# A batched matmul with hardware loops on ScalarE and VectorE, and transfer completions passed on by GpSimd

## The chip, the cores and the metric

One core of one Trainium2 chip. The metric is the device time of the whole kernel in microseconds (us), lower is better.

## The reference

```python
batch, m, k, n = 16, 512, 512, 512          # a: (16,512,512) f32, b: (16,512,512) f32
def reference(a, b):
    return np.matmul(a, b.transpose(0, 2, 1)).astype(np.float32)
```

Inputs are 33.55 MB, the output 16.78 MB, all f32 in HBM.

## The kernel before

The sixteen products are worked in eight pairs. SP loads `a` and `b` of a pair (2 MiB each) into seven slots; VectorE casts each load to bf16 in two halves (`h` and `w`), TensorE transposes both through PSUM, ScalarE copies the transposed `a` out (`ta`), VectorE the transposed `b` (`tb`), TensorE multiplies, ScalarE copies the result to one of seven output slots (`ob`), and SP stores it (1 MiB). TensorE already runs a hardware loop. ScalarE and VectorE are unrolled; each wait names an absolute count. Store 0 alone goes out from ScalarE's own transfer queue (q10 in the page: 1.05 MB).

```python
ORDER = "LLLLLLLSLLLLSLSSLSLSLLSSSSSSSSS"    # SP: L = a load, S = a store (from store 1 on)
# ... SP
if n_ld >= NL:
    nc.sync.wait_ge(s_cd, n_ld - NL + 1)     # the slot's last cast is done
# ... the first two loads come in two halves; VectorE casts half by half
# VectorE, unrolled over pairs u
nc.vector.wait_ge(s_ld[n % NL], 16 * (n // NL + 1))
nc.vector.wait_ge(s_t, KO * u)
nc.vector.tensor_copy(out=h[:], in_=src[:, :, :HK]).then_inc(s_c, 1)
nc.vector.tensor_copy(out=w[:], in_=src[:, :, HK:]).then_inc(s_cd, 1)
# ... then ha<-wa, tb, hb<-wb, tb, tb, tb
# ScalarE, unrolled over pairs
nc.scalar.wait_ge(s_mm, J * i + j + 1)
c = nc.scalar.copy(out=ob[i % NO][:, j, :]..., in_=ps[:, j, :]...)
if i == 1 and j == 0:
    nc.scalar.wait_ge(s_out, 1)
    nc.scalar.dma_start(out[0]..., ob[0][:]).then_inc(s_st[0], 16)
```

Of the kernel before, what the change touches and what calls it, by code (L numbers as in the profile page):

```python
# [10 lines left out]
def kernel(  # L11
# [6 lines left out]
    nc = tc.nc  # L18
    P = 128
    batch, M, K = a.shape  # L20
    _, N, _ = b.shape
    J = M // P
    KO = K // P
    HP = P // 2
    HK = K // 2
    pairs = batch // 2
    f32 = mybir.dt.float32
    bf16 = mybir.dt.bfloat16
    NL = 7
    NO = 7  # L30


    ORDER = "LLLLLLLSLLLLSLSSLSLSLLSSSSSSSSS"

    def sbuf(name, shape, dtype):
        return ctx.enter_context(nc.sbuf_tensor(name, shape, dtype))

    def sem(name):
        return tc.alloc_semaphore(name)

    with tc.tile_critical(no_gpsimd_drain=True):  # L41
        ident = sbuf("ident", [P, P], bf16)
        ld = [sbuf(f"ld{i}", [P, 2 * J, K], f32) for i in range(NL)]
        ha, wa, hb, wb = (
            sbuf(name, [P, 2 * J, HK], bf16) for name in ("ha", "wa", "hb", "wb")
        )
        ta = sbuf("ta", [P, KO, 2 * J * P], bf16)
        tb = sbuf("tb", [P, KO, 2 * J * P], bf16)
        ob = [sbuf(f"ob{i}", [P, J, N], f32) for i in range(NO)]
        tp = ctx.enter_context(nc.psum_tensor("tp", [P, 4, 2 * J, P], bf16))  # L50
        ps = ctx.enter_context(nc.psum_tensor("ps", [P, 4, N], f32))

# [1 line left out]
        s_ld = [sem(f"s_ld{i}") for i in range(NL)]  # L54
        s_second = [sem(f"s_second{i}") for i in range(2)]
        s_st = [sem(f"s_st{i}") for i in range(NO)]
        s_cd = sem("s_cd")
        s_ca = sem("s_ca")
        s_cb = sem("s_cb")
        s_ta = sem("s_ta")  # L60
        s_tb = sem("s_tb")
        s_ea = sem("s_ea")
        s_eb = sem("s_eb")
        s_mm = sem("s_mm")
        s_pv = sem("s_pv")
        s_out = sem("s_out")
# [5 lines left out]
            out=ident[:], in_=ident[:], compare_op=mybir.AluOpType.not_equal, fill=1.0,  # L72
# [4 lines left out]



        n_ld, n_st = 0, 1  # L80
        for what in ORDER:
            if what == "L":
                u, slot = n_ld // 2, n_ld % NL
                src = (a if n_ld % 2 == 0 else b)[2 * u:2 * u + 2].rearrange(
                    "e (p j) k -> (e p) j k", j=2 * J
                )
                if n_ld >= NL:

                    nc.sync.wait_ge(s_cd, n_ld - NL + 1)
                if n_ld < 2:  # L90
                    nc.sync.dma_start(
                        ld[slot][:, :J, :], src[:, :J, :]
                    ).then_inc(s_ld[slot], 16)
                    nc.sync.dma_start(
                        ld[slot][:, J:, :], src[:, J:, :]
                    ).then_inc(s_second[slot], 16)
                else:
                    nc.sync.dma_start(ld[slot][:], src).then_inc(s_ld[slot], 16)
                n_ld += 1
            else:  # L100
                slot = n_st % NO
                nc.sync.wait_ge(s_out, n_st + 1)
                nc.sync.dma_start(
                    out[n_st].rearrange("(p j) n -> p j n", j=J), ob[slot][:]
                ).then_inc(s_st[slot], 16)
                n_st += 1
        for n in range(batch - NO, batch - 1):
            nc.sync.wait_ge(s_st[n % NO], 16 * (n // NO + 1))




        nc.vector.nop().then_inc(s_eb, 2)
        nc.vector.wait_ge(s_set, 2)
        both = ((ha, wa, s_ca, s_ta), (hb, wb, s_cb, s_tb))
        for u in range(pairs):
            for x, (h, w, s_c, s_t) in enumerate(both):
                n = 2 * u + x
                src = ld[n % NL]
                nc.vector.wait_ge(s_ld[n % NL], 16 * (n // NL + 1))  # L120
                nc.vector.wait_ge(s_t, KO * u)
                if n >= 2:
                    nc.vector.tensor_copy(out=h[:], in_=src[:, :, :HK]).then_inc(s_c, 1)  # L123
                    nc.vector.tensor_copy(out=w[:], in_=src[:, :, HK:]).then_inc(s_cd, 1)  # L124
                else:
                    nc.vector.tensor_copy(out=h[:, :J, :], in_=src[:, :J, :HK])  # L126
                    nc.vector.tensor_copy(out=w[:, :J, :], in_=src[:, :J, HK:])  # L127
                    nc.vector.wait_ge(s_second[n], 16)
                    nc.vector.tensor_copy(  # L129
                        out=h[:, J:, :], in_=src[:, J:, :HK]  # L130
                    ).then_inc(s_c, 1)
                    nc.vector.tensor_copy(  # L132
                        out=w[:, J:, :], in_=src[:, J:, HK:]
                    ).then_inc(s_cd, 1)
            for ko in range(KO):
                if ko < 2:
                    h, w, s_c, s_t = both[ko]
                    nc.vector.wait_ge(s_cd, 2 * u + ko + 1)
                    nc.vector.wait_ge(s_t, KO * u + 2)
                    nc.vector.tensor_copy(out=h[:], in_=w[:]).then_inc(s_c, 1)  # L140
                nc.vector.wait_ge(s_tb, KO * u + ko + 1)
                nc.vector.tensor_copy(  # L142
                    out=tb[:, ko, :],
                    in_=tp[:, 2 + ko % 2].rearrange("k j p -> k (j p)"),
                ).then_inc(s_eb, 1)


        nc.scalar.nop().then_inc(s_ea, 2)
        for u in range(pairs):
            for ko in range(KO):  # L150

                nc.scalar.wait_ge(s_ta, KO * u + ko + 1)
                for e in range(2):
                    c = nc.scalar.copy(  # L154
                        out=ta[:, ko, e * J * P:(e + 1) * J * P].rearrange(
                            "k (j p h) -> k j p h", j=J, h=2
                        ),
                        in_=tp[:, ko % 2, :, e * HP:(e + 1) * HP].rearrange(
                            "k (h j) p -> k j p h", h=2
                        ),  # L160
                    )
                c.then_inc(s_ea, 1)
            for e in range(2):
                i = 2 * u + e
                if i >= NO:
                    nc.scalar.wait_ge(s_st[i % NO], 16 * (i // NO))
                for j in range(J):
                    nc.scalar.wait_ge(s_mm, J * i + j + 1)

                    c = nc.scalar.copy(  # L170
                        out=ob[i % NO][:, j, :].rearrange("m (p j) -> m p j", j=2 * J),
                        in_=ps[:, j, :].rearrange("m (j p) -> m p j", j=2 * J),
                    )
                    if j == J - 1:
                        c.then_inc(s_out, 1)
                    elif e == 0 or j == 0:
                        c.then_inc(s_pv, 1)
                    if i == 1 and j == 0:
                        nc.scalar.wait_ge(s_out, 1)
                        nc.scalar.dma_start(  # L180
                            out[0].rearrange("(p j) n -> p j n", j=J), ob[0][:]
                        ).then_inc(s_st[0], 16)


        def take(s, n):
            nc.tensor.wait_ge(s, n).then_inc(s, -n)  # L186

        pe = nc.tensor.engine
        with nc.Fori(0, pairs, engines=[pe]):
            with nc.Fori(0, 2, engines=[pe]):  # L190

                for x, (h, s_c, s_t, s_e) in enumerate(
                    ((ha, s_ca, s_ta, s_ea), (hb, s_cb, s_tb, s_eb))
                ):
                    take(s_c, 1)
                    for g in range(2):
                        take(s_e, 1)
                        for j in range(2 * J):
                            t = nc.tensor.transpose(  # L199
                                tp[:, 2 * x + g, j, :], h[:, j, g * P:(g + 1) * P], ident[:]  # L200
                            )
                        t.then_inc(s_t, 1)
            nc.tensor.wait_ge(s_ea, 2)
            nc.tensor.wait_ge(s_eb, 2)


            for e in range(2):
                for j in range(J):
                    if e == 1 and j % 2 == 0:
                        take(s_pv, 2)  # L210
                    for ko in range(KO):
                        t = nc.tensor.matmul(  # L212
                            ps[:, j, :],
                            ta[:, ko, (e * J + j) * P:(e * J + j + 1) * P],
                            tb[:, ko, :].rearrange("k (j p) -> k j p", j=2 * J)[
                                :, :, e * HP:(e + 1) * HP
                            ],
                            start=(ko == 0),
                            stop=(ko == KO - 1),
                        )  # L220
                    t.then_inc(s_mm, 1)
# [34 lines left out]
```

## Time and profile before

| | before |
|---|---|
| time, median of the first 3 runs | 126.25 us |
| span of the profiled run | 124.3 us |
| busy: TensorE, VectorE, ScalarE | 74%, 55%, 57% |
| transfer engines | 9 tenths in all slices but the first and the last two |
| last output copy ends | 115.43 us |
| last store: issued, landed on the slowest engine | 115.46, 123.02 us |

In the profile's rows PE is TensorE (PEld its weight loads), DVE VectorE, ACT ScalarE, POOL GpSimd and SP SyncE; a q behind the name (SPq, DVEq) is the engine's sequencer or queue, L129 a line of the kernel. Each transfer runs in sixteen parts on sixteen transfer engines (each of the 34 issues in this trace has sixteen landing records). "Landing" is the record that a part has arrived, and "rings" are the queues in which issued transfers wait for the engines: the median store of this trace lands 24.7 us after its issue.

The rows that carry this are shown in the prediction. The two columns to hold side by side are the last two lines of the table: compute ends 7.6 us before the transfers do.

Two rows of the timeline show how the first pair starts (columns: start us, length us, engine, line, operation, output from input, count, idle time before it and what ended it):

```profile
8.52 0.69 DVE L129 CAST ha<-ld 128x1024 bf16<-128x1024 f32 x1 [1.11 <-DMA ld<-in_a_dram]
14.70 0.69 DVE L140 COPY ha<-wa 128x2048 bf16<-128x2048 bf16 x1
```

The second half of the first `a` landed at 8.49 us, so its cast begins 0.03 us later.

### The profile page before, as it was taken

Reading aid. Unit: us, or ns where it says so; the run is one execution under the profiler, and the core shown is the slowest. Engines: PE = TensorE matmul, PEld = TensorE weight load, DVE = VectorE, ACT = ScalarE, POOL = GpSimd, SP = SyncE. Lnnn points to the kernel's source line nnn. Section 1 sums busy time; section 2 is a strip of 40 time slices with the busy share of each in tenths; the row PEclk is TensorE's granted clock in tenths of the full one; section 3 lists DMA queues with packets and bytes.
Section 4 is the critical chain, followed back from the end, with each engine's and each line's share of the span. In section 5 each row is a group of like instructions: output and inputs, shape, how many; then the busy total and the mean of one; then the engine's idle time right before and its main releaser. Section 6 shows DMA issues by size and latency. Waiting matters only on the chain. (4 is left out here: it accounts for less than half of the span.)

```text
span 124.3 us, 2076 instructions
## 1 busy us (share of the span) xinstructions
PE 91.8 (74%) x768; PEld 56.5 (45%) x768; DVE 67.9 (55%) x84; ACT 71.0 (57%) x129; POOL 0.7 (1%) x6
## 2 busy tenths in 40 slices
PE   0005397998699869986998699869986998699000
PEld 0005394447444744574447444744474447443000
DVE  0065668827891788278907890782686568400000
ACT  4006042769476946694669476947694769476100
POOL 2000000000000000000000000000000000000000
PEclk9999999999999999999999999999999999999955
DMA  3999999999999999999999999999999999999980
GB/s 79 403 427 451 443 427 427 427 427 374 411 427 424 445 432 443 424 422 430 414 430 406 416 451 387 403 451 416 448 427 422 419 422 427 427 427 427 424 377 34
DMA packets 4898, 50.35 MB, mean 405 GB/s; under 512 B 544, under 2 KB 544, under 8 KB 544
## 3 DMA queue, kind: packets, MB, share of 16 engines
q1 hardware_dynamic: 4752, 49.29, 94.5%
q10 hardware_dynamic: 144, 1.05, 2.0%
q14 instruction: 2, 0.02, 0.0%
HBM read 33.55 MB, written 16.78 MB: 405 GB/s over the span
## 5 line engine op out<-in xcount | busy, mean ns | idle before, releaser
L212 PE MATMUL ps<-tb,ta 128*128 128x512 bf16 x256 | 57.3, 379 | 8.0 <-DVE tb L142 8.0
L170 ACT COPY ob<-ps 128x512 f32<-128x512 f32 x64 | 37.6, 587 | 30.1 <-PE ps L212 30.1
L212 PEld LDWEIGHTS ps<-tb,ta 128*128 128x128 bf16 x256 | 23.9, 97 | 39.0 <-ACT ta L154 8.2
L154 ACT COPY ta<-tp 128x512 bf16<-128x512 bf16 x64 | 32.9, 604 | 13.3 <-PE tp L199 12.9
L199 PE MATMUL tp<-ident,ha 128*128 128x128 bf16 x256 | 19.7, 230 | 11.8 <-PEq L186 10.9
L199 PEld LDWEIGHTS tp<-ident,ha 128*128 128x128 bf16 x256 | 16.7, 104 | 15.5 <-issue 13.8
L142 DVE COPY tb<-tp 128x1024 bf16<-128x1024 bf16 x32 | 21.3, 685 | 3.9 <-PE tp L199 3.6
L199 PE MATMUL tp<-ident,hb 128*128 128x128 bf16 x256 | 18.5, 230 | 3.1 <-PEq L186 3.1
L199 PEld LDWEIGHTS tp<-ident,hb 128*128 128x128 bf16 x256 | 16.3, 104 | 3.4 <-issue 3.3
L140 DVE COPY ha<-wa 128x2048 bf16<-128x2048 bf16 x8 | 5.5, 693 | 18.1 <-PE tp L199 18.1
L123 DVE CAST hb<-ld 128x2048 bf16<-128x2048 f32 x7 | 8.6, 1226 | 7.2 <-DMA ld<-in_b_dram 7.2
L123 DVE CAST ha<-ld 128x2048 bf16<-128x2048 f32 x7 | 8.5, 1219 | 0.6 <-DMA ld<-in_a_dram 0.6
L124 DVE CAST wb<-ld 128x2048 bf16<-128x2048 f32 x7 | 8.5, 1221 | 0.0
L124 DVE CAST wa<-ld 128x2048 bf16<-128x2048 f32 x7 | 8.5, 1220 | 0.0
L140 DVE COPY hb<-wb 128x2048 bf16<-128x2048 bf16 x8 | 5.5, 685 | 0.2 <-PE tp L199 0.2
L126 DVE CAST ha<-ld 128x1024 bf16<-128x1024 f32 x1 | 0.7, 694 | 6.1 <-DMA ld<-in_a_dram 6.1
L154 ACT ACT_TABLE_LOAD x1 | 1.3, 1283 | 1.0 <-SPq L41 1.0
L129 DVE CAST hb<-ld 128x1024 bf16<-128x1024 f32 x1 | 0.7, 694 | 1.2 <-DMA ld<-in_b_dram 1.2
L126 DVE CAST hb<-ld 128x1024 bf16<-128x1024 f32 x1 | 0.7, 695 | 1.2 <-DMA ld<-in_b_dram 1.2
L129 DVE CAST ha<-ld 128x1024 bf16<-128x1024 f32 x1 | 0.7, 694 | 1.1 <-DMA ld<-in_a_dram 1.1
L132 DVE CAST wa<-ld 128x1024 bf16<-128x1024 f32 x1 | 0.7, 689 | 0.0
L127 DVE CAST wa<-ld 128x1024 bf16<-128x1024 f32 x1 | 0.7, 687 | 0.0
(8 smaller groups left out, 2.3 us busy)
## 6 DMA issues: line engine op xcount, KB each, us to landing
out_dram<-ob SPq DMA_DIRECT2D x15, 1024.0 KB, 25.8
ld<-in_a_dram SPq DMA_DIRECT2D x7, 2048.0 KB, 30.8
ld<-in_b_dram SPq DMA_DIRECT2D x7, 2048.0 KB, 30.5
ld<-in_a_dram SPq DMA_DIRECT2D x2, 1024.0 KB, 6.1
ld<-in_b_dram SPq DMA_DIRECT2D x2, 1024.0 KB, 10.1
out_dram<-ob ACTq DMA_DIRECT2D x1, 1024.0 KB, 12.2
```

The lines of the kernel that those rows point to most:

```text
L123: nc.vector.tensor_copy(out=h[:], in_=src[:, :, :HK]).then_inc(s_c, 1)
L124: nc.vector.tensor_copy(out=w[:], in_=src[:, :, HK:]).then_inc(s_cd, 1)
L126: nc.vector.tensor_copy(out=h[:, :J, :], in_=src[:, :J, :HK])
L127: nc.vector.tensor_copy(out=w[:, :J, :], in_=src[:, :J, HK:])
L129: nc.vector.tensor_copy(out=h[:, J:, :], in_=src[:, J:, :HK]).then_inc(s_c, 1)
L132: nc.vector.tensor_copy(out=w[:, J:, :], in_=src[:, J:, HK:]).then_inc(s_cd, 1)
L140: nc.vector.tensor_copy(out=h[:], in_=w[:]).then_inc(s_c, 1)
L142: nc.vector.tensor_copy(out=tb[:, ko, :], in_=tp[:, 2 + ko % 2].rearrange("k j p -> k (j p)"),).then_inc(s_eb, 1)
L154: c = nc.scalar.copy(out=ta[:, ko, e * J * P:(e + 1) * J * P].rearrange("k (j p h) -> k j p h", j=J, h=2), in_=tp[:, ko % 2, :, e * HP:(e ...
L170: c = nc.scalar.copy(out=ob[i % NO][:, j, :].rearrange("m (p j) -> m p j", j=2 * J), in_=ps[:, j, :].rearrange("m (j p) -> m p j", j=2 * J),)
L199: t = nc.tensor.transpose(tp[:, 2 * x + g, j, :], h[:, j, g * P:(g + 1) * P], ident[:])
L212: t = nc.tensor.matmul(ps[:, j, :], ta[:, ko, (e * J + j) * P:(e * J + j + 1) * P], tb[:, ko, :].rearrange("k (j p) -> k j p", j=2 * J)[:, ...
```

## The change

The intent is a much smaller program for ScalarE and VectorE: one loop body each instead of eight copies. This loop body is the same code for every pair and names neither the semaphore of a slot nor a growing count, so GpSimd waits for the real completions in issue order and passes them on as plain counts (`s_go` for loads, `s_of` for free output slots), and each consumer takes its count back off the semaphore. Slots are addressed from a register. A tiny copy ahead of ScalarE's loop is to make the activation table load there and not in the loop. Store 0 is issued once, ScalarE's loop body runs for every pair, so it moves to SP's queue, ahead of store 1.

```diff
-    ORDER = "LLLLLLLSLLLLSLSSLSLSLLSSSSSSSSS"
+    ORDER = "LLLLLLLSSLLLLSLSSLSLSLLSSSSSSSSS"
-        n_ld, n_st = 0, 1
+        n_ld = n_st = 0
-                    nc.sync.wait_ge(s_cd, n_ld - NL + 1)
+                    nc.sync.wait_ge(s_cd, n_ld - NL + 2)
 # GpSimd, new
+        for what in ORDER:
+            if what == "L":
+                if n_ld < 2:
+                    nc.gpsimd.wait_ge(s_second[n_ld], 16)
+                nc.gpsimd.wait_ge(s_ld[n_ld % NL], 16 * (n_ld // NL + 1)).then_inc(s_go, 1)
+            else: ...  # the same for stores, s_st -> s_of
+        def taker(engine):
+            return lambda s, n: engine.wait_ge(s, n).then_inc(s, -n)
 # VectorE
-        for u in range(pairs):
+        with nc.Fori(0, pairs, engines=[dve]) as u:
+                src = ld[:, bass.ds((u * 2 + x) % NL, 1)]...
+                take(s_go, 1)
+                if x == 0:
+                    take(s_da, 1)
-                    nc.vector.tensor_copy(out=w[:], in_=src[:, :, HK:]).then_inc(s_cd, 1)
+                nc.vector.tensor_copy(out=w[:, :J, :], in_=src[:, :J, HK:]).then_inc(s_cd, 1)
+                nc.vector.tensor_copy(out=w[:, J:, :], in_=src[:, J:, HK:]).then_inc(s_w, 1)
 ...
 # ScalarE
+        nc.scalar.copy(out=one[:], in_=nc.const_aps.tensor(1.0, (P, 1), f32))
-        for u in range(pairs):
+        with nc.Fori(0, pairs, engines=[act]) as u:
+            take(s_of, 2)
+                dst = ob[:, bass.ds((u * 2 + e) % NO, 1)]...
-                    if i == 1 and j == 0:
-                        nc.scalar.wait_ge(s_out, 1)
-                        nc.scalar.dma_start(out[0]..., ob[0][:]).then_inc(s_st[0], 16)
 # TensorE: the first hb transpose of a round also raises s_da, which VectorE takes
+                            if x == 1 and g == 0 and j == 0:
+                                t.then_inc(s_da, 1)
```

More of the change, by code (lines that the diff above doesn't have):

```diff
@@ L42 @@
         ident = sbuf("ident", [P, P], bf16)
-        ld = [sbuf(f"ld{i}", [P, 2 * J, K], f32) for i in range(NL)]
+        one = sbuf("one", [P, 1], f32)
+        ld = sbuf("ld", [P, NL, 2 * J, K], f32)
         ha, wa, hb, wb = (
@@ L48 @@
         tb = sbuf("tb", [P, KO, 2 * J * P], bf16)
-        ob = [sbuf(f"ob{i}", [P, J, N], f32) for i in range(NO)]
+        ob = sbuf("ob", [P, NO, J, N], f32)
         tp = ctx.enter_context(nc.psum_tensor("tp", [P, 4, 2 * J, P], bf16))
@@ L56 @@
         s_st = [sem(f"s_st{i}") for i in range(NO)]
+        s_go = sem("s_go")
+        s_of = sem("s_of")
         s_cd = sem("s_cd")
+        s_wa = sem("s_wa")
+        s_wb = sem("s_wb")
         s_ca = sem("s_ca")
         s_cb = sem("s_cb")
+        s_da = sem("s_da")
         s_ta = sem("s_ta")
@@ L87 @@
                 if n_ld >= NL:
-                    nc.sync.wait_ge(s_cd, n_ld - NL + 1)
+                    nc.sync.wait_ge(s_cd, n_ld - NL + 2)
                 if n_ld < 2:
                     nc.sync.dma_start(
-                        ld[slot][:, :J, :], src[:, :J, :]
+                        ld[:, slot, :J, :], src[:, :J, :]
                     ).then_inc(s_ld[slot], 16)
                     nc.sync.dma_start(
-                        ld[slot][:, J:, :], src[:, J:, :]
+                        ld[:, slot, J:, :], src[:, J:, :]
                     ).then_inc(s_second[slot], 16)
                 else:
-                    nc.sync.dma_start(ld[slot][:], src).then_inc(s_ld[slot], 16)
+                    nc.sync.dma_start(ld[:, slot], src).then_inc(s_ld[slot], 16)
                 n_ld += 1
@@ L103 @@
                 nc.sync.dma_start(
-                    out[n_st].rearrange("(p j) n -> p j n", j=J), ob[slot][:]
+                    out[n_st].rearrange("(p j) n -> p j n", j=J), ob[:, slot]
                 ).then_inc(s_st[slot], 16)
@@ L108 @@
             nc.sync.wait_ge(s_st[n % NO], 16 * (n // NO + 1))
+        n_ld = n_st = 0
+        for what in ORDER:
[3 more added lines that the diff above has]
+                nc.gpsimd.wait_ge(s_ld[n_ld % NL], 16 * (n_ld // NL + 1)).then_inc(s_go, 1)
+                n_ld += 1
+            else:
+                if n_st < batch - NO:
+                    nc.gpsimd.wait_ge(
+                        s_st[n_st % NO], 16 * (n_st // NO + 1)
+                    ).then_inc(s_of, 1)
+                n_st += 1
@@ L113 @@
+        def taker(engine):
+            return lambda s, n: engine.wait_ge(s, n).then_inc(s, -n)
+        dve = nc.vector.engine
+        take = taker(nc.vector)
         nc.vector.nop().then_inc(s_eb, 2)
+        nc.vector.nop().then_inc(s_da, 1)
         nc.vector.wait_ge(s_set, 2)
-        both = ((ha, wa, s_ca, s_ta), (hb, wb, s_cb, s_tb))
-        for u in range(pairs):
-            for x, (h, w, s_c, s_t) in enumerate(both):
-                n = 2 * u + x
-                src = ld[n % NL]
-                nc.vector.wait_ge(s_ld[n % NL], 16 * (n // NL + 1))
-                nc.vector.wait_ge(s_t, KO * u)
-                if n >= 2:
-                    nc.vector.tensor_copy(out=h[:], in_=src[:, :, :HK]).then_inc(s_c, 1)
-                    nc.vector.tensor_copy(out=w[:], in_=src[:, :, HK:]).then_inc(s_cd, 1)
-                else:
-                    nc.vector.tensor_copy(out=h[:, :J, :], in_=src[:, :J, :HK])
-                    nc.vector.tensor_copy(out=w[:, :J, :], in_=src[:, :J, HK:])
-                    nc.vector.wait_ge(s_second[n], 16)
-                    nc.vector.tensor_copy(
-                        out=h[:, J:, :], in_=src[:, J:, :HK]
-                    ).then_inc(s_c, 1)
-                    nc.vector.tensor_copy(
-                        out=w[:, J:, :], in_=src[:, J:, HK:]
-                    ).then_inc(s_cd, 1)
-            for ko in range(KO):
-                if ko < 2:
-                    h, w, s_c, s_t = both[ko]
-                    nc.vector.wait_ge(s_cd, 2 * u + ko + 1)
-                    nc.vector.wait_ge(s_t, KO * u + 2)
-                    nc.vector.tensor_copy(out=h[:], in_=w[:]).then_inc(s_c, 1)
-                nc.vector.wait_ge(s_tb, KO * u + ko + 1)
@@ new lines @@
+        with nc.Fori(0, pairs, engines=[dve]) as u:
+            for x, (h, w, s_c, s_w) in enumerate(
+                ((ha, wa, s_ca, s_wa), (hb, wb, s_cb, s_wb))
+            ):
+                src = ld[:, bass.ds((u * 2 + x) % NL, 1)].rearrange("p o j k -> p (o j) k")
+                take(s_go, 1)
+                if x == 0:
+                    take(s_da, 1)
+                nc.vector.tensor_copy(out=h[:], in_=src[:, :, :HK]).then_inc(s_c, 1)
+                nc.vector.tensor_copy(
+                    out=w[:, :J, :], in_=src[:, :J, HK:]
+                ).then_inc(s_cd, 1)
+                nc.vector.tensor_copy(
+                    out=w[:, J:, :], in_=src[:, J:, HK:]
+                ).then_inc(s_w, 1)
+            for ko in range(KO):
+                if ko == 0:
+                    take(s_wa, 1)
+                    take(s_da, 1)
+                    nc.vector.tensor_copy(out=ha[:], in_=wa[:]).then_inc(s_ca, 1)
+                take(s_tb, 1)
+                if ko == 1:
+                    take(s_wb, 1)
+                    nc.vector.tensor_copy(out=hb[:], in_=wb[:]).then_inc(s_cb, 1)
@@ L145 @@
                 ).then_inc(s_eb, 1)
+        act = nc.scalar.engine
+        take = taker(nc.scalar)
         nc.scalar.nop().then_inc(s_ea, 2)
-        for u in range(pairs):
+        nc.scalar.nop().then_inc(s_of, NO)
+        nc.scalar.copy(out=one[:], in_=nc.const_aps.tensor(1.0, (P, 1), f32))
+        with nc.Fori(0, pairs, engines=[act]) as u:
             for ko in range(KO):
-                nc.scalar.wait_ge(s_ta, KO * u + ko + 1)
+                if ko < KO - 1:
+                    nc.scalar.wait_ge(s_ta, ko + 1)
+                else:
+                    take(s_ta, KO)
                 for e in range(2):
@@ L162 @@
                 c.then_inc(s_ea, 1)
+            take(s_of, 2)
             for e in range(2):
-                i = 2 * u + e
-                if i >= NO:
-                    nc.scalar.wait_ge(s_st[i % NO], 16 * (i // NO))
+                dst = ob[:, bass.ds((u * 2 + e) % NO, 1)].rearrange("m o j n -> m (o j) n")
                 for j in range(J):
-                    nc.scalar.wait_ge(s_mm, J * i + j + 1)
+                    if j < J - 1:
+                        nc.scalar.wait_ge(s_mm, j + 1)
+                    else:
+                        take(s_mm, J)
                     c = nc.scalar.copy(
-                        out=ob[i % NO][:, j, :].rearrange("m (p j) -> m p j", j=2 * J),
+                        out=dst[:, j, :].rearrange("m (p j) -> m p j", j=2 * J),
                         in_=ps[:, j, :].rearrange("m (j p) -> m p j", j=2 * J),
@@ L177 @@
                         c.then_inc(s_pv, 1)
-                    if i == 1 and j == 0:
-                        nc.scalar.wait_ge(s_out, 1)
-                        nc.scalar.dma_start(
-                            out[0].rearrange("(p j) n -> p j n", j=J), ob[0][:]
-                        ).then_inc(s_st[0], 16)
-        def take(s, n):
-            nc.tensor.wait_ge(s, n).then_inc(s, -n)
         pe = nc.tensor.engine
+        take = taker(nc.tensor)
         with nc.Fori(0, pairs, engines=[pe]):
```

## The prediction

> **What bounds the kernel now.** I read the page first (DMA rows, then queues), then the table of stretches, then the queue's own waits, then the timeline of the last two pairs. The page says:
>
> ```profile
> DMA  3999999999999999999999999999999999999980
> GB/s 79 403 427 451 443 427 427 427 427 374 411 427 424 445 432 443 424 422 430 414 430 406 416 451 387 403 451 416 448 427 422 419 422 427 427 427 427 424 377 34
> q1 hardware_dynamic: 4752, 49.29, 94.5%
> q10 hardware_dynamic: 144, 1.05, 2.0%
> HBM read 33.55 MB, written 16.78 MB: 405 GB/s over the span
> PE 91.8 (74%) x768; PEld 56.5 (45%) x768; DVE 67.9 (55%) x84; ACT 71.0 (57%) x129; POOL 0.7 (1%) x6
> ```
>
> The reader is to see that the sixteen transfer engines are at 9 tenths in every slice but the first and the last two, while no compute engine is above 74%. The stretches, in finer steps (columns: stretch, length, busy time of the five engines, granted clock, DMA share, GB/s):
>
> ```profile
> 0.00:3.00 3.00, 0.00 (x0) 0.00 (x0) 0.00 (x0) 1.28 (x1) 0.70 (x6) 1.00 0.31 71
> 20.00:60.00 40.00, 35.34 (x299) 21.13 (x300) 28.04 (x34) 26.99 (x50) 0.00 (x0) 1.00 1.01 424
> 60.00:100.00 40.00, 35.94 (x302) 21.28 (x301) 25.07 (x30) 27.86 (x52) 0.00 (x0) 1.00 1.00 422
> 116.00:121.00 5.00, 0.00 (x0) 0.00 (x0) 0.00 (x0) 0.00 (x0) 0.00 (x0) 0.75 0.96 406
> ```
>
> The DMA share is 1.00 from 3 us to 116 us, and in 116:121 the transfers go on at 0.96 with all compute over. So the time is bytes over rate: 16 loads of 2 MiB and 16 stores of 1 MiB are 48 units of 1 MiB. In the landing records one unit takes 2.45 us in the quiet early stretch (landings at 6.02, 8.49, 10.97, 13.46 us), so 48 units are about 117.7 us. With the first unit's start, 6.02 - 2.45 = 3.6 us, that makes 121.3. The last landing is at 123.02: the other 1.7 us are drift between the sixteen engines. The sixteen parts of one transfer land within 0.7 us of each other early (17.69 to 18.36) and within 2.3 us at the end (120.74 to 123.02), and the slowest engine sets the end. From there to the end of the span are 1.3 us, and from span to measured time 126.1 - 124.3 = 1.8 us. The change moves neither bytes nor packet sizes.
>
> The question is then whether compute can become late enough to leave the transfer engines idle. The only place where it nearly could is the last store:
>
> ```profile
> SPq L103 <- ACT ob L170: 99.9, 15, 22.6
> DMA to landing us min/median/max: 7.6/24.7/37.3
> 95.17 7.19 PE L212 MATMUL ps<-tb,ta 128*128 128x512 bf16 x32 [1.02 <-DVE tb L142]
> 102.19 1.06 PE L199 MATMUL tp<-ident,ha 128*128 128x128 bf16 x16
> 103.35 0.69 DVE L140 COPY ha<-wa 128x2048 bf16<-128x2048 bf16 x1 [0.51 <-PE tp L199]
> 106.19 1.29 DVE L142 COPY tb<-tp 128x1024 bf16<-128x1024 bf16 x2 [0.34 <-PE tp L199]
> 107.62 7.18 PE L212 MATMUL ps<-tb,ta 128*128 128x512 bf16 x32 [1.02 <-DVE tb L142]
> 114.84 0.59 ACT ob L170
> ```
>
> The first line is the SP queue waiting for ScalarE; it looks bad (99.9 us) but costs nothing, since a typical transfer still waits about 25 us in the rings (second line, stores only). The minimum, 7.6 us, is the last store, issued at 115.46. The timeline rows under it show the rhythm: matmul start to matmul start is 107.62 - 95.17 = 12.45 us per pair, and the last copy (a row of the chain) ends at 115.43. A pair's traffic is 6 units, 14.7 us. So compute starts at 9.5 us, runs at its own 12.45 us without ever running the rings dry, and ends ahead of the transfers.
>
> **How much ahead.** The last store's last packet ends at 122.54; eight packets of 0.309 us are 2.47, so the slowest engine began it at 120.07. From issue to packets took 1.0 us for the first engine and about 1.8 us for the last one, at the first load (issued 0.94, packets from 1.95 to 2.7). So the last store may be issued as late as 120.07 - 1.8 = 118.3 to 120.07 - 1.0 = 119.1: slack 2.8 to 3.6 us. I use 3.2. Beyond that each us of compute delay is a us of time.
>
> [...] the page's slices sit at 424 to 427 on the plateaus[...] this trace has one load of 1283 ns, at 0.98 us, where ScalarE idles anyway. [...] TensorE's loop in this trace is my measure: one ALU record of 36 ns and one branch of about 208 ns per turn.
>
> **The change, part by part.**
>
> 1. The first two loads are no longer cast by halves. Before: second half of the first `a` lands 8.49, cast of the half 0.69, first transpose at 9.5. After: a GpSimd hop (estimate 0.1 us, no such hop is in the trace), then a full cast of 1.22 us: about +0.6. The same for `b` (lands 13.46), and the second-half casts wait behind the longer first one: hb from 13.56 to about 14.8, then two half casts at 0.6 to 0.7 to about 16.0, so the copy ha<-wa starts near 15.95 instead of 14.70. First-pair delay: about +1.2 us, once.
>
> 2. Counted waits. Each removed wait rode on its instruction or was a 21 ns record; each new one is a record of 17 (ACT), 21 (DVE) ns with about 0.07 us to the next start. Where the engine still runs the copy before, it is hidden. Three lie on the chain of each transpose phase: ha<-wa now waits for the first hb transpose instead of the last ha one (estimate 0.06 us: their ends differ by that[...]), then dispatch after that wait and after the one before the third tb copy (estimate 0.05 each). About 0.15 us per pair, 1.2 us for eight.
>
> 3. Loop turns on ScalarE and VectorE: 36 + 208 ns by TensorE's example, plus the slot arithmetic. VectorE's falls where it has slack: casts of about 5 us in a matmul phase of 7.2 us. ScalarE's falls between its last ob copy (102.39, 0.59 long) and the first ta copy (102.87); the sequencer can turn while the copy runs, and ScalarE ends ta at 107.04 against VectorE's 107.48. I add 0 to 0.1 us per pair.
>
> 4. wa/wb casts split: 2 x 0.61 spaced instead of 1.14 apart, about +0.1 us per load, in the slack of the matmul phase: 0 on the path.
>
> 5. Loads wait for one cast more. Load 10, for instance (counting from 0), waits for load 4's cast near 35 us instead of load 3's near 26; at that time some 10 MiB are still queued ahead (the rest of load 6, two stores, loads 7 to 9). 0.
>
> 6. GpSimd passes landings in issue order, and the rings serve in issue order: 0 beyond the hop. Store slots for the last pair need stores 7 and 8, landed at 105.45, against a first ob copy at 108.73: 0.
>
> 7. The first store leaves ScalarE's queue: the slices around 28 to 35 us dip to 374 GB/s, and load 5 came late because two queues alternated, but the six units 28.16 to 43.17 took 15.0 us against 14.7. At most -0.3, perhaps part of the drift.
>
> Sum on compute: 1.2 + 1.2 + about 0.4 = 2.8 us (plausible 1.5 to 4.5), end of compute near 118.2. Against slack 3.2: hidden, with a few tenths showing at the unlucky side. Sum on transfers: -0.3 to 0. Net: about -0.1 to +0.3.
>
> **Rivals.** (a) The loops cost more than TensorE's: code refetched at each turn, or register addresses slow every ob copy. For: nothing on these engines has been looped here. Against: TensorE's far longer body turns in 0.2 us, and each ob copy has 0.28 us idle before it. With 0.6 us a pair more, compute is 7 us late and the time is about 130. (b) The table load falls inside the loop after all: 8 x 1.28 = 10 us late, less 3.2, time about 133; the added copy ahead of the loop is there to prevent it. (c) The delay just exceeds the slack: 4.5 - 3.2 = 1.3 us, 127.5. I hold this for the likeliest miss. (d) Faster: only if drift of the slowest engine shrinks with one queue and fewer instruction fetches (two of 0.31 us at 50.1 and 58.7 us hit single engines): 125.5, not below 123.7, which 2% would need.
>
> **Range and chances.** 126.2 us; 125.5 is rival (d) in full, 127.6 is (c) in full. Slower by 2% means 128.8, compute over 5.7 us late: (a) or (b), together 6%. Faster by 2% would need fewer bytes: 1%. The rest, 93%, is within 2%.
>
> **What would show it.** Right: DMA share 1.00 from 3 to 116 us again; first transposes near 10.1 us; matmul start to start 12.5 to 12.7 us; the last ob copy ending at 117 to 119 us and the shortest store issue-to-landing down from 7.6 to some 4 to 6 us; one table load. Step 1 is wrong if the first matmul starts elsewhere than 21.5 to 22; step 2 or 3 if the pair takes over 12.8 us. The prediction as a whole is wrong if the DMA share falls below 0.9 before 118 us.

## The result, and the profile after

The changed kernel took 127.0 us (median of 4 runs, 126.96 to 127.19), the kernel before 126.4 us (4 runs, 126.08 to 126.59) beside it. Ratios in this document are the mean time of one kernel's fast runs over that of the other's of the same rounds, so not quite the ratio of the medians (in the experiments the profiled runs are left out of it): here 1.0054, with a 95% interval of 1.0027 to 1.0080. That is within 2%, inside the predicted range, and 0.8 us above the predicted 126.2. The question for the experiments is where some 0.5% came from.

The page of the changed kernel, the rows that answer to those of before:

```profile
DMA  3999999999999999999999999999999999999880
GB/s 84 408 434 442 442 424 429 424 419 439 434 317 416 445 403 429 424 434 424 421 453 408 398 450 403 411 447 413 455 445 419 405 421 437 416 421 419 374 369 18
q1 hardware_dynamic: 4896, 50.33, 96.1%
HBM read 33.55 MB, written 16.78 MB: 402 GB/s over the span
PE 91.6 (73%) x768; PEld 55.7 (44%) x768; DVE 68.3 (55%) x96; ACT 71.0 (57%) x130; POOL 0.7 (1%) x6
```

The same bytes go through the same engines, still saturated, now on one queue (there is no second queue row). Two things differ: slice 12 (34.5 to 37.6 us) moves only 317 GB/s although the engines count as busy, and the last slices are less full. By stretches:

```profile
20.00:60.00 40.00, 33.93 (x291) 20.36 (x292) 27.22 (x39) 26.25 (x49) 0.00 (x0) 1.00 1.01 419
60.00:100.00 40.00, 34.98 (x298) 20.76 (x296) 27.10 (x39) 26.80 (x50) 0.00 (x0) 1.00 1.01 425
116.00:121.00 5.00, 1.88 (x8) 0.68 (x8) 0.00 (x0) 1.75 (x3) 0.00 (x0) 1.00 0.86 359
```

From 116 to 121 us there is now compute work, and the DMA share is 0.86 where it was 0.96: some transfer engines ran dry and waited for the last store. The rows of the stores' landing, of the last two pairs, and the last row of the chain:

```profile
DMA to landing us min/median/max: 5.2/23.5/36.0
97.81 7.27 PE L242 MATMUL ps<-tb,ta 128*128 128x512 bf16 x32 [1.14 <-DVE tb L168]
104.92 1.06 PE L227 MATMUL tp<-ident,ha 128*128 128x128 bf16 x16
106.18 0.69 DVE L163 COPY ha<-wa 128x2048 bf16<-128x2048 bf16 x1 [2.41 <-DVEq L133]
109.17 1.29 DVE L168 COPY tb<-tp 128x1024 bf16<-128x1024 bf16 x2 [0.50 <-DVEq L133]
110.61 7.27 PE L242 MATMUL ps<-tb,ta 128*128 128x512 bf16 x32 [1.14 <-DVE tb L168]
118.08 0.58 ACT ob L205
```

Matmul start to matmul start is 110.61 - 97.81 = 12.80 us (12.45 before). The last copy ends at 118.66 instead of 115.43: compute is 3.2 us later. The last store is issued at 118.69 and lands 5.2 us later instead of 7.6. "DVEq L133" as releaser means that VectorE's own sequencer was in the taking wait (line 133 is the helper `taker`).

It is tempting to read the story off at once: the last store came 3.2 us late, engines ran dry, time rose. The landing records contradict it. On the slowest of the sixteen engines store 14 landed at 121.48 us and store 15 at 123.92, 2.44 us apart, the length of one store: that engine never waited. In the kernel before, the same two moments are 120.52 and 123.02. The slowest engine was already 1 us behind before the last store mattered.

The first pair after the change:

```profile
8.91 1.23 DVE L152 CAST ha<-ld 128x2048 bf16 x1 [8.91 <-DVEq L133]
16.12 0.69 DVE L163 COPY ha<-wa 128x2048 bf16<-128x2048 bf16 x1
```

The landing is at 8.47 us, the cast starts 0.44 us later (0.03 before), and the copy ha<-wa at 16.12 instead of 14.70.

### The profile page after: what moved, and what is told of

Read it like the earlier page. It is cut to its first block, busy times and chain, and to the rows that moved or that the text cites.

```text
span 125.3 us, 2349 instructions
## 1 busy us (share of the span) xinstructions
PE 91.6 (73%) x768; PEld 55.7 (44%) x768; DVE 68.3 (55%) x96; ACT 71.0 (57%) x130; POOL 0.7 (1%) x6
## 5 line engine op out<-in xcount | busy, mean ns | idle before, releaser
L205 ACT COPY ob<-ps 128x512 f32 x64 | 37.5, 585 | 33.0 <-PE ps L242 27.3
L227 PE MATMUL tp<-ident,hb 128*128 128x128 bf16 x256 | 17.8, 225 | 3.0 <-PEq L133 3.0
L227 PEld LDWEIGHTS tp<-ident,hb 128*128 128x128 bf16 x256 | 15.8, 102 | 3.2 <-issue 3.2
L152 DVE CAST ha<-ld 128x2048 bf16 x8 | 9.8, 1221 | 8.9 <-DVEq L133 8.9
L152 DVE CAST hb<-ld 128x2048 bf16 x8 | 9.8, 1225 | 6.4 <-DVEq L133 6.4
L156 DVE CAST wb<-ld 128x1024 bf16 x8 | 5.5, 688 | 0.0
L153 DVE CAST wb<-ld 128x1024 bf16 x8 | 5.5, 688 | 0.0
L156 DVE CAST wa<-ld 128x1024 bf16 x8 | 5.5, 688 | 0.0
L153 DVE CAST wa<-ld 128x1024 bf16 x8 | 5.5, 687 | 0.0
L178 ACT ACT_TABLE_LOAD x1 | 1.3, 1283 | 1.1 <-SPq L41 1.1
```

The lines of the kernel that those rows point to most:

```text
L153: nc.vector.tensor_copy(out=w[:, :J, :], in_=src[:, :J, HK:]).then_inc(s_cd, 1)
L156: nc.vector.tensor_copy(out=w[:, J:, :], in_=src[:, J:, HK:]).then_inc(s_w, 1)
L178: nc.scalar.copy(out=one[:], in_=nc.const_aps.tensor(1.0, (P, 1), f32))
L205: c = nc.scalar.copy(out=dst[:, j, :].rearrange("m (p j) -> m p j", j=2 * J), in_=ps[:, j, :].rearrange("m (j p) -> m p j", j=2 * J),)
L227: t = nc.tensor.transpose(tp[:, 2 * x + g, j, :], h[:, j, g * P:(g + 1) * P], ident[:])
```

## The experiments

Theories. **T**: the late last store cost the time. **Q**: moving store 0 from ScalarE's queue to SP's cost the time, in the transfers. **N**: mostly chance, since single runs of the kernel before spread from 125.7 to 127.8 us. Twelve experiments ran (e5, e6 and e9 repeat an earlier kernel), all gave right results. Kernels of one round share the runs of the kernel before on their chip, so ratios of one round are not independent of each other. e9 to e11 ran a round later than e5 to e8 and are set against the same eleven runs of the kernel before and one more; within their own round e10 and e11 are 0.2% and 0.4% above e9. One run of the kernel before fell to a granted clock of 0.603 and took 176.72 us, and is left out.

| run | store 0 from | compute late | median us | before beside it | ratio, 95% interval | GB/s from 24 to 48 us | load 7 landed, us |
|---|---|---|---|---|---|---|---|
| before (first profile) | ScalarE | no | | | | 421 | 48.06 |
| changed (first profile) | SP | 3 us | 127.0 | 126.4 | 1.0054 (1.0027 to 1.0080) | 411 | 48.97 |
| e1_store0_sp | SP | no | 127.25 | 126.86 | 1.0019 (0.9977 to 1.0062) | 411 | 49.24 |
| e2_late4 | ScalarE | 3 us, end only | 126.68 | 126.86 | 0.9981 (0.9942 to 1.0020) | 415 | 48.62 |
| e3_late8 | ScalarE | 6 us, end only | 128.68 | 126.86 | 1.0134 (1.0095 to 1.0174) | 421 | 48.50 |
| e4_store0_act | ScalarE | 3 us | 126.89 | 126.86 | 1.0000 (0.9956 to 1.0044) | 416 | 48.76 |
| e5_after_again | SP | 3 us | 127.21 | 126.81 | 1.0026 (1.0003 to 1.0049) | 404 | 49.52 |
| e6_store0_sp_again | SP | no | 127.55 | 126.81 | 1.0055 (1.0026 to 1.0083) | 409 | 49.26 |
| e7_fewer_turns | ScalarE | no | 126.52 | 126.81 | 0.9991 (0.9967 to 1.0015) | 421 | 48.52 |
| e8_no_preload | SP | much | 146.95, low clock | 126.81 | none | 411 | 49.33 |
| e9_store0_act_again | ScalarE | 3 us | 126.79 | 126.79 | 1.0004 (0.9975 to 1.0033) | 420 | 48.51 |
| e10_dve_unrolled | SP | 2.7 us | 126.99 | 126.79 | 1.0026 (0.9993 to 1.0059) | 408 | 49.17 |
| e11_act_unrolled | SP | 2.2 us | 127.29 | 126.79 | 1.0049 (1.0018 to 1.0080) | 410 | 49.53 |
| e12_store0_sp_early | SP, early | no | 126.87 | 126.32 | 1.0053 (1.0016 to 1.0090) | 421 | 49.38 |

"Load 7 landed" is the last of its sixteen parts in the landing records; by then the same loads and stores have gone through in every variant (loads 0 to 7, stores 0 and 1), whichever of them went first. Where compute is marked as not late, the last store was issued between 115.46 and 116.56 us: in some of these traces the casts of a late pair wait for a load (in e6 the matmuls of the seventh pair start 13.80 us after those of the sixth, not 12.45).

### e1_store0_sp: only store 0 moved

```diff
-    ORDER = "LLLLLLLSLLLLSLSSLSLSLLSSSSSSSSS"
+    ORDER = "LLLLLLLSSLLLLSLSSLSLSLLSSSSSSSSS"
-        n_ld, n_st = 0, 1
+        n_ld, n_st = 0, 0
-                    if i == 1 and j == 0:
-                        nc.scalar.wait_ge(s_out, 1)
-                        nc.scalar.dma_start(...)
```

> The kernel before, with one change: store 0 goes out from the SP queue behind load 6, right ahead of store 1, as in the changed kernel; no loop, no counted wait. Theory Q (the 0.7 us come from the transfers themselves: in the changed trace the slowest engine's last store follows its store 14 without a gap, 121.48 to 123.92, so lateness of the last store cannot have cost it anything; what differs is that store 0 no longer runs on a second queue beside loads 5 and 6): about 127.0 us, with the last store still issued near 115.5 and 7 us or more from issue to landing. Theory T (the 0.7 us come from the last store, issued 3.2 us later at 118.7, after which faster engines idle up to 1.3 us): 126.3 us, as before.

Measured 127.25 us against 126.86, ratio 1.0019 with an interval that holds both 1.0 and 1.0054: by its time alone it settles nothing. Its trace does show a difference. Stretch from 24 to 48 us, first the kernel before, then this run (columns as in the stretches above; the last is GB/s):

```profile
24.00:48.00 24.00, 21.29 (x190) 13.01 (x189) 16.12 (x20) 16.83 (x31) 0.00 (x0) 1.00 1.01 421
```

```profile
24.00:48.00 24.00, 21.29 (x190) 13.00 (x188) 16.05 (x20) 16.87 (x32) 0.00 (x0) 1.00 1.01 411
```

The compute columns are alike, the share is 1.01 in both, and 10 GB/s are missing: 24 us x 10 GB/s = 0.24 MB, which at 427 GB/s is 0.56 us. The lower rate of the changed kernel is there without any loop. These are single traces, but the table's columns agree: 404 to 411 GB/s in all seven with store 0 late in SP's queue, 415 to 421 in all six with it in ScalarE's.

### e2_late4 and e3_late8: only the last store late

```diff
                     nc.scalar.wait_ge(s_mm, J * i + j + 1)
+                    if i == batch - 1 and j == J - 1:
+                        nc.scalar.wait_ge(s_pad, 1)
+                        for x in range(4):                 # 8 in the second kernel
+                            nc.scalar.copy(out=scr[:, x, :], in_=pad[:])
```

> The kernel before, with four extra copies of 128x768 on ScalarE ahead of the very last output copy, about 3 us, so that only the last store is issued late, near 118.5, as in the changed kernel (the extra copies go to a scratch tile; results stay right). Theory T: about 127.0 us. Theory Q: 126.3 us, unchanged, the last store taking about 4.5 to 5 us from issue to landing. My prediction's slack of 3.2 us says the same as Q here.

> The same with eight extra copies, about 6 us, last store issued near 121.5. Both theories: later than before, as the slack is used up. By the prediction's slack of 2.8 to 3.6 us it should be 126.3 + 6 - 3.2 = 129 us (128.5 to 129.5); if the true slack is only about 2.5 us, as T has it, 129.8. This calibrates the slack.

The timeline of the first of them, and its row of stores' landing:

```profile
115.31 3.03 ACT L176 CAST scr<-pad 128x768 uint8<-128x768 bf16 x4 [0.28 <-PE ps L220]
118.84 0.33 SPq L107 DMA_DIRECT2D out_dram<-ob  x1
DMA to landing us min/median/max: 4.5/25.7/38.5
```

The last store was issued at 118.84, as late as in the changed kernel, and the time was 126.68 against 126.86. Theory T expected about 0.7 us more. It falls. With eight copies:

```profile
115.33 5.96 ACT L176 CAST scr<-pad 128x768 uint8<-128x768 bf16 x8 [0.28 <-PE ps L220]
121.80 0.33 SPq L107 DMA_DIRECT2D out_dram<-ob  x1
DMA to landing us min/median/max: 3.8/25.5/38.4
```

Here the store meets empty engines: 3.8 us from issue to landing is what a 1 MiB store takes alone. The time rises by 1.34%, 1.7 us, for 5.9 us of lateness (the eight copies start at 115.33 and the last output copy at 121.20), and by 1.9 to 2.0 us against the run with four copies. The slack is therefore about 4 us, a little more than the 2.8 to 3.6 predicted. The trace of before says the same: 123.02 - 3.8 = 119.2 is the latest harmless issue, 3.7 us after 115.46.

### e4_store0_act and e9_store0_act_again: the change, with store 0 back on ScalarE's queue

```diff
-        with nc.Fori(0, pairs, engines=[act]) as u:
-            ...
+        def act_pair(u, peeled): ...                       # the same body
+                    if peeled and e == 1 and j == 0:
+                        nc.scalar.wait_ge(s_out, 1)
+                        nc.scalar.dma_start(out[0]..., ob[:, 0]).then_inc(s_st[0], 16)
+        act_pair(0, True)
+        with nc.Fori(1, pairs, engines=[act]) as u:
+            act_pair(u, False)
 # SP: starts with store 1, one S fewer in its order
```

> The changed kernel, with ScalarE's first pair taken out of its loop (same code, static slot) so that store 0 can be issued from ScalarE's queue as before; loops over the other seven pairs, counted waits and GpSimd's counts stay, so compute stays about 3 us late. Theory Q: the 0.7 us go away, about 126.3 us. Theory T: they stay, about 127.0 us.

> The changed kernel with store 0 back on ScalarE's queue (first pair of ScalarE ahead of its loop), again, since the first result had an interval of 0.9%. So far all four comparisons with store 0 in SP's queue gave +0.2 to +0.55% against the kernel before and all three with store 0 in ScalarE's queue gave -0.2 to 0.0%. Theory Q: 0.0%, within 0.2% of the kernel before, though the last copy still ends 3 us later. Theory N: as the changed kernel, +0.3 to +0.5%.

Ratios 1.0000 and 1.0004. Compute is as late as in the changed kernel: in the second run's trace the matmuls still start 12.79 us apart and the last copy ends at 119.2. The stretch from 24 to 48 us of the second run:

```profile
24.00:48.00 24.00, 20.77 (x187) 12.79 (x186) 15.70 (x23) 16.59 (x31) 0.00 (x0) 1.00 1.01 420
```

With the loops, the counted waits and GpSimd's counts all in place, but store 0 on ScalarE's queue, no loss is seen. Neither interval alone excludes the changed kernel's +0.26% of the other round, but with e2 and e7 four ratios of four with that queue lie between 0.9981 and 1.0004.

### e5_after_again and e6_store0_sp_again: the same two, for the spread

The changed kernel and e1, unedited, five rounds each.

> The changed kernel itself once more, beside the next two on one chip, because the kernel before spread from 126.1 to 127.8 us over eleven runs, which is as much as the 0.7 us to be explained. Theory N (most of the 0.7 us was chance: four runs against four): within 0.3 us of the kernel before. Theory Q (store 0 behind load 6 in SP's queue costs transfer time): 0.4 to 0.7 us above it, and level with the next run.

> The kernel before with store 0 in SP's queue, again, since its first result (+0.4 us, interval -0.3 to +0.8) settled nothing. Theory Q: 0.3 to 0.5 us above the kernel before again, and level with the changed kernel. Theory N: level with the kernel before.

Ratios 1.0026 and 1.0055, both intervals above 1. Theory N explains at most a part: all seven ratios with store 0 in SP's queue lie between 1.0019 and 1.0055 (mean 1.0040, about 0.5 us), all four with it in ScalarE's, leaving out the deliberately late e3, between 0.9981 and 1.0004. The changed kernel's stretch in this run:

```profile
24.00:48.00 24.00, 20.66 (x187) 12.66 (x185) 15.42 (x23) 16.29 (x31) 0.00 (x0) 1.00 1.01 404
```

### e7_fewer_turns: fewer turns from writing to reading

```diff
-    ORDER = "LLLLLLLSLLLLSLSSLSLSLLSSSSSSSSS"
+    ORDER = "LLLLLLLSLLLLLLSSSLLLSSSSSSSSSSS"
```

> The kernel before with its loads and stores in longer rows: after store 0 and 1 six loads, then stores 2 to 4, then three loads, then stores 5 to 15, so that the transfers turn from writing to reading two times instead of six. In all traces so far packets longer than the usual 309 or 611 ns are gathered at the first store (near 28 or 36 us) and right after the turns to loads (44, 66, 76 us); after the start they add up to about 20 to 30 us over sixteen engines, 1.3 to 1.9 us for each. If the turns cause them (the ground of theory Q), this saves 0.3 to 0.8 us, unless the later stores 5 and 6 hold ScalarE up by more than the slack of 3 to 4 us. If they come at fixed moments whatever the order, the time is unchanged, about 126.5 to 126.9.

126.52 against 126.81, ratio 0.9991 (0.9967 to 1.0015): no gain is shown, and the expected 0.3 to 0.8 us is largely excluded (the interval allows at most 0.4 us). So no gain from turning less often is seen, although slow packets do gather after turns (in the changed kernel 4.6, 2.6 and 2.9 us of excess start in the two us from 44, 66 and 76 us). What its packets take over the usual length adds up to 27.8 us against 28.5 in the kernel before, over sixteen engines, in one trace each; without the first 4 us it is 15.5 against 20.0, 0.3 us an engine, too little to be told in these times. This was the only candidate for a version that beats both kernels, and it does not clearly do so.

### e8_no_preload: the table load left inside the loop

```diff
-        nc.scalar.copy(out=one[:], in_=nc.const_aps.tensor(1.0, (P, 1), f32))
```

> The changed kernel without the copy ahead of ScalarE's loop, so that the table load falls inside it (the compiled order shows it there, ahead of the first ta copy). 8 loads of 1.28 us in place of one. By my rival (b): seven of them on the path, 9 us of compute lateness more on top of the 3.2 us, so the last copy ends near 127 to 128 us and the time is 127 + 9 less the slack still left, 0 to 1 us: about 135 us. If the loads hid behind ScalarE's idle time before its first ta copy: 127 to 129 us.

The four runs took 140.64 to 151.52 us at granted clocks of 0.861 to 0.948, against about 0.98 otherwise, so the time can't be compared with fast runs; I expected about 135. What can be read is the pair in the part of the trace where the clock was still full:

```profile
43.26 1.06 PE L226 MATMUL tp<-ident,ha 128*128 128x128 bf16 x16
44.23 1.28 ACT L186 ACT_TABLE_LOAD   x1
57.46 1.06 PE L226 MATMUL tp<-ident,ha 128*128 128x128 bf16 x16
58.43 1.28 ACT L186 ACT_TABLE_LOAD   x1
```

Pair to pair is 57.46 - 43.26 = 14.20 us, 1.4 more than the changed kernel's 12.80: the load of 1.28 us stands on the path in full (the next copy starts 1.29 us after the load began, 59.72 - 58.43). From 58 us on the granted clock drops:

```profile
28.00:58.00 30.00, 23.84 (x208) 14.37 (x207) 16.92 (x24) 20.74 (x37) 0.00 (x0) 1.00 1.00 416
58.00:100.00 42.00, 33.10 (x259) 19.28 (x257) 23.00 (x33) 26.25 (x45) 0.00 (x0) 0.84 1.00 424
```

Whether the reloads brought the low clock on is open; the kernel before showed a low clock once as well (0.603). The copy ahead of the loop is needed in any case, for the 1.4 us a pair.

### e10_dve_unrolled and e11_act_unrolled: where the 0.35 us of a pair sit

```diff
 # e10: VectorE, the same instructions in the same order
-        with nc.Fori(0, pairs, engines=[dve]) as u:
+        for u in range(pairs):
-                take(s_go, 1)                 # and so on
+                nc.vector.wait_ge(s_go, n + 1)
 # e11: ScalarE likewise, static ob slots
```

> The changed kernel with VectorE unrolled: the same casts and copies in the same order, but static slots and waits on absolute counts instead of waits that take. The pair is 12.80 us in the changed kernel against 12.45. If the takes on VectorE's chain cost what I read from the trace (0.10 for the copy ha<-wa and 0.15 to 0.16 up to the third tb copy), the matmul start to start falls to 12.5 to 12.6 and the last copy ends about 116.8. The time: by theory Q unchanged, 127.0 to 127.2, since compute is off the path.

> The changed kernel with ScalarE unrolled: static slots, absolute counts, no register operation ahead of each output copy. If these operations (46 to 106 ns each in the changed trace) hold back TensorE's matmuls through the output copies, the matmul phase falls from 7.27 to 7.19 us and the pair from 12.80 to about 12.71. The time: by theory Q unchanged, 127.0 to 127.2.

Matmul start to matmul start falls from 12.79 to 12.68 us with VectorE unrolled and to 12.61 with ScalarE unrolled. One matmul row of each, e10 first:

```profile
97.41 7.27 PE L241 MATMUL ps<-tb,ta 128*128 128x512 bf16 x32 [1.03 <-DVE tb L167]
```

```profile
97.24 7.13 PE L233 MATMUL ps<-tb,ta 128*128 128x512 bf16 x32 [1.14 <-DVE tb L168]
```

The first cast of e10, where GpSimd still passes the landing on but VectorE has neither takes nor slot arithmetic:

```profile
8.63 1.23 DVE L151 CAST ha<-ld 128x2048 bf16<-128x2048 f32 x1 [8.63 <-POOLq L123]
```

It starts 0.12 us after the landing at 8.51, where the changed kernel needs 0.44.

VectorE's takes and slot arithmetic cost 0.11 us a pair, all in the transpose phase (the wait before the matmuls falls from 1.14 to 1.03); I had expected 0.2 to 0.3, and the last copy at 116.8 us instead of the 118.2 measured. ScalarE's part is larger, 0.18, and 0.14 of it is in the matmul row, 7.27 to 7.13; I had expected 0.08. The likely cause is in ScalarE's records of the changed kernel, first the operations on registers (count, then shortest, median and longest ns), then what its output copies waited for (us in total, times, longest):

```profile
L205 ACTq FUSED_REGOPS  x64: 46/46/117, 22.1 to 118.0; - x64
ACT ob L205 <- PE ps L242: 27.3, 48, 2.1
ACT ob L205 <- ACTq L133: 5.7, 16, 0.4
```

Each output copy is preceded by an operation that computes its slot's address, after the wait for its matmul and not before it, and every fourth copy waits in the take. The program lets TensorE write a tile of `ps` again only when these copies have raised `s_pv`. In the last pair of the changed trace the copy that raises it ends at 115.85 us and TensorE takes it at 115.89; its matmuls there start 0.42 us apart (115.57, 115.99) where the others are 0.22 apart, and in the kernel before 0.34 (112.58, 112.92). e11 removed addresses and takes together, so how they share the 0.18 us is not shown. 0.11 + 0.18 = 0.29 of 0.35 us; the other 0.06 is the later release of ha<-wa. The trace of e10, without takes, shows it: from the start of the first ha transposes to ha<-wa it is 105.74 - 104.52 = 1.22 us, in the kernel before 103.35 - 102.19 = 1.16. The times, 126.99 and 127.29, stay at the changed kernel's, as they should if compute is off the path.

### e12_store0_sp_early: the queue or the place

```diff
 # on top of e1
-    ORDER = "LLLLLLLSSLLLLSLSSLSLSLLSSSSSSSSS"
+    ORDER = "LLLLLSLLSLLLLSLSSLSLSLLSSSSSSSSS"
```

> As the run with store 0 in SP's queue, but SP holds loads 5 and 6 back until store 0 is issued near 25.5 us, so that the one queue carries load 4, store 0, loads 5 and 6, store 1. So far store 0 differed in two things at once: the queue, and the place (early beside loads 5 and 6, or late behind load 6 and right ahead of store 1). Theory Q-place: the late place costs; here the time is that of the kernel before, within 0.2%, and the stretch from 24 to 48 us moves 415 to 421 GB/s. Theory Q-queue: one queue for the first store costs; here +0.4% as with store 0 behind load 6, and 404 to 411 GB/s in that stretch.

The two signs disagree. The time says queue: 1.0053 (1.0016 to 1.0090). The rate says place:

```profile
24.00:48.00 24.00, 21.29 (x190) 13.03 (x189) 16.13 (x20) 16.81 (x31) 0.00 (x0) 1.00 1.01 421
```

The landing records show how both can be. The first part of load 7 lands at 47.34 us, as early as ever (47.42 in the kernel before), but the last at 49.38: the sixteen engines are 2.0 us apart, against 0.6 in the kernel before, 1.0 to 1.3 in the other five traces with store 0 in ScalarE's queue and 1.3 to 1.9 in those with it late in SP's. Mean rate was recovered, evenness was not, and the slowest engine ends the kernel. So by the time it is the single queue that counts, as far as one experiment shows, and the mean GB/s is not a sure sign to go by. This is one trace, and its own run was a quick one (126.47 us), so the split between a rate part and an evenness part is not settled. Two rivals stay: e12 also issues loads 5 and 6 at 25.2 and 25.7 us instead of near 5, and its store 0 lands by 31.06 us, ahead of load 5, where on a second queue it alternated with load 5 and landed at 37.26. No run had store 0 late on ScalarE's queue.

## Why the prediction was right or wrong

**What bounds it: right.** The transfers set the end in every run but e3 and e8. The DMA share from 3 to 116 us is unchanged (and 0.95 from 116 to 118, above the 0.9 that I had named as the sign of being wrong), the time within 0.6%.

**The slack: right in kind, too small.** Predicted 2.8 to 3.6 us, measured about 4 by e2 and e3. The term of the sum that was mis-sized is the 1.0 to 1.8 us from issue to packets, taken from the very first load, when several issues start together; the lone store of e3 has its first packets 0.83 us after its issue (121.80 to 122.63) and takes 3.8 us in all.

**Step 1, first pair: the hop was right, what follows it was left out.** I put 0.1 us for GpSimd, my estimate with no trace behind it, and e10 shows about that: 0.12 us from landing to cast. In the changed kernel it is 0.44 us instead of 0.03, as two takes of VectorE (their records start at 8.54 and 8.65) and a register operation of 118 ns for the slot come between. ha<-wa starts at 16.12 where I had 15.95. The first matmul moved by only 0.47 us in the first pair of traces (20.59 to 21.06), outside the 21.5 to 22 that I had named, but by 1.6 us between e6 (19.87) and e5 (21.47) of one chip. What differs is when TensorE speeds up: sixteen transposes take 1.87 us at first and 1.06 later, and the last set ahead of the first matmul took 1.87 in the trace of before and 1.16 in that of after. In the kernel before, the transposes start 106 to 107 ns apart in the set at 17.84 us and 55 to 56 in the one at 27.56. The granted clock of the profile reads 1.00 in the stretch with the slow ones (3 to 20 us), so only the starts and durations show it.

**Steps 2 and 3: mis-sized.** 0.15 and 0 to 0.1 us a pair, measured 0.35. VectorE's take at the third tb copy and at ha<-wa came out near the 0.1 that I gave them together (0.11 in e10). The 0.06 us for the later release of ha<-wa is what the trace of e10 shows. The miss is ScalarE: I looked at its loop turn, which is short and hidden (records of 35, 45 and 35 ns while a copy runs; VectorE's has 40, 56 and 36), and not at the address that each output copy now computes after its wait (an operation of 46 to 117 ns), or at the take ahead of every fourth. I had even written in rival (a) that 0.28 us of idle time before each copy would swallow the address; that idle time is the wait for TensorE, the operation comes behind it, and the copies hold TensorE back in turn.

**Steps 4, 5 and 6: no cost is seen, as written** (e4 and e9 have all three and show no loss); load 10 was issued at 35.47 us, with the rings full (it landed at 63.59). That they serve in issue order, as step 6 has it, shows in the landing records of both first traces: the last parts of SP's transfers, 33 before and 34 after, land in the order of their issue.

**The sum on compute** was 2.8 us, measured 3.2 (115.43 to 118.66), hidden as predicted. That it came so close is luck: in this pair of traces only 0.47 of my 1.2 us for the first pair reached the first matmul, since TensorE was fast sooner, and my 1.6 us for the eight pairs were 2.8; the two errors cancel. (In the rivals the sums left this base out in part: 0.6 us a pair more makes 2.8 + 4.8 = 7.6 us, not 7, and eight table loads 2.8 + 10.2 = 13 us, not 10.)

**The net and step 7, the step that failed.** I forecast -0.1 to +0.3 us against the kernel before and it was about +0.6 (0.5%); the range held the result only because it allowed for rival (c). The step behind this is step 7: "The first store leaves ScalarE's queue ... At most -0.3, perhaps part of the drift." The sign was wrong. It costs about 0.4%, 0.5 us, and within the intervals it is the whole measured difference: e1 and e6 have it without the loops, e4 and e9 have the loops without it. In six of the seven runs with store 0 in SP's queue it also goes later in the order, so only e12 (1.0053) speaks for the queue alone. I had seen that load 5 landed late in the trace of before, where two queues alternate (from 29 to 34 us 84 packets of SP's queue start and 82 of ScalarE's), and took that for a loss; it was only a different order of landing. Rival (c), a delay beyond the slack, which I held for the likeliest miss and which the top of the range stood for, did not happen.

**Left open**: why the first store costs more in SP's queue than on a second queue. In the late place the slow packets come in the 2 us ahead of the first store's packets (34.8 to 36.9 us in the changed kernel, about 11 us of excess over the sixteen engines; about 7 us between 27 and 33 in the kernel before). The other traces agree: packets that start between 24 and 38 us have 11 to 14 us of excess in all seven with store 0 late in SP's queue and 4 to 9 in all six with it in ScalarE's, a difference of about 0.4 us an engine, most of the 0.5 us. In e12 this excess is gone (5 us) and the time is not, which leaves the spread of the engines or another cause.

## What to carry to other kernels

In this kernel, bound by transfers, a compute engine's lateness was free up to a slack that can be measured: issue-to-landing of the last transfer, less what such a transfer takes alone (7.6 - 3.8 = 3.8 us; about 4 by e2 and e3). When a small regression appears with a late last store beside it, look at the slowest engine's landings before blaming the store; undoing each part alone here cleared the loops and convicted a side effect of the rewrite. In a loop body, count on the time of an address computed behind a wait (here an operation of 46 to 126 ns, and with the takes 0.11 us a pair on VectorE and 0.18 on ScalarE; to compute it ahead of the wait is the obvious remedy, which no run here tried), and load tables before the loop (1.4 us a pair in e8).
